# The root of every norm as one power on GpSimd, in a hybrid decoder layer

## The chip, the core and the metric

The kernel runs on one core of a Trainium2 chip. A core has five engines with their own instruction queues: TensorE (PE in the profile; its weight loads are PEld), VectorE (DVE), ScalarE (ACT), GpSimd (POOL) and SyncE (SP), which here issues the DMAs. Each queue is worked off in order, and queues wait for each other through semaphores. The metric is the device time of one execution in microseconds (us); lower is better.

## The reference

One decoder layer on x of 1024 tokens by 1024 channels: a gated feed-forward half step, a mixer of two head groups (a gated short convolution and a diagonal state space model), a second feed-forward half step, and a final norm. What matters here is that every part starts with a root mean square norm over the channels of a token:

```python
def rms_norm(x, gain):
    xf = x.astype(jnp.float32)
    y = xf * lax.rsqrt(jnp.mean(xf * xf, axis=-1, keepdims=True) + EPS)
    return (y * gain.astype(jnp.float32)).astype(x.dtype)

x = x + 0.5 * g1 * swiglu(modulate(rms_norm(x, ffn1_norm), sh1, sc1), ...)
h = modulate(rms_norm(x, mix_norm), sh2, sc2)          # -> conv branch, ssm branch
y_mix = concatenate([rms_norm(y_conv, out_norm_conv), rms_norm(y_ssm, out_norm_ssm)])
x = x + g2 * (y_mix @ w_out)
x = x + 0.5 * g3 * swiglu(modulate(rms_norm(x, ffn2_norm), sh3, sc3), ...)
return rms_norm(x, final_norm)
```

So there are six norms: before the first feed-forward, before the mixer, one for each head group's output, before the second feed-forward, and at the end. Each needs one value per token, 1/sqrt(mean + 1e-6).

## The kernel before

Channels lie on the 128 partitions and tokens along the free axis, in two halves of 512 tokens. Every matrix product is done with both operands split into a high and a low part (three matmuls per product, `mm3`), so TensorE has some 7500 matmuls of 128x128 by 512. Weights come by DMA into `raw`, ScalarE casts the high part `w`, VectorE subtracts to get the low part; GpSimd adds and subtracts weight blocks (`sums`, `raw`) for the blocks that are multiplied with seven products instead of eight.

A norm goes through five steps, each on another engine. ScalarE squares the channel tiles, GpSimd and VectorE add the squares (tiles named `..q`); TensorE multiplies the sum with a column of ones, which leaves the sum of squares of 512 tokens as 128 partitions by 4 columns in `st`; `roots` turns `st` into the inverse root `y` (128x4); `wide` copies each column of `y` 128 times into `rb` (128x512); `spread` multiplies `rb` with the identity on TensorE, so that `bc` holds the root of each token on all partitions; then VectorE multiplies the channel tiles with `bc`. `Sumsq.rstd` puts `stats` (the sums, `roots` and `wide`) a few ticks behind its cause, and `spread` another 7 or 11 ticks behind that; one tick is one `mm3`. These are the due times by which the author places the steps between the matmuls.

`roots` on VectorE before the change: one instruction makes v = st/width + eps (`..nv`). Then eight small ones on 128x4: a first guess from the bits of v as an integer (`ni`), and two polynomial steps (`na`, `ny`), the last of which leaves y larger by 1/0.375; the factor 0.375 is applied in `wide`.

There are 13 calls. Two are in the prologue (`root_of(0)` and `root_of(1)`, names `p0..` and `p1..`), where the tokens lie on the partitions and the result `py` is used by ScalarE and GpSimd themselves to scale the token rows `xb`, before TensorE transposes them (`pt`); there a ninth small instruction multiplies by 0.375. Then one for each half: `n2a`, `n2b` (mixer norm), `nAa`, `nAb` (convolution output), `nBa`, `nBb` (state space output), `n3a`, `n3b` (second feed-forward). The final norm has three: `n_0_0` for the first half, and `n_1_0` and `n_1_256` for two quarters of the second (the profile cuts the numbers and shows them as `n_0..` and `n_256..`).

The order on each engine is that of the source in the prologue (`InOrder.strict`); behind it a scheduler orders the instructions of each engine by their dependences and its own estimate of durations. A long side job shares the engines with the matmuls: 56 products of a weight tile `wm` with the condition vector (`mod_tile`, one VectorE instruction of 128x1024 and one accumulator read), each of which frees one of two buffers and so lets SyncE issue the next `wm` load.

Of the kernel before, what the change touches and what calls it, by code (L numbers as in the profile page):

```python
# [13 lines left out]
F32 = mybir.dt.float32  # L14
F32R = mybir.dt.float32r
I32 = mybir.dt.int32
AF = mybir.ActivationFunctionType
ALU = mybir.AluOpType
# [3 lines left out]
P = 128  # L22
D = 1024
# [29 lines left out]
RC2 = float(np.float32(np.round((TWO_PI - RC1) * 2.0**20) / 2.0**20))  # L53
RC3 = float(np.float32(TWO_PI - RC1 - RC2))
ROUND = 12582912.0
ROOT_BITS, ROOT_A, ROOT_B = 1595932665.0, 0.703952253, 2.38924456
EXP_C = [1.9875691500e-4, 1.3981999507e-3, 8.3334519073e-3, 4.1665795894e-2, 1.6666665459e-1, 5.0000001201e-1]


# [176 lines left out]
def hymba_layer(ctx: ExitStack, tc, x_d, xt_d, wm1_d, wmod_d, gu1_d, gs1_d, ds1_d, wl1_d, win_d, wout_d, glu_d, gu2_d, gs2_d, wd2_d, ds2_d, wl2_d, cols_d, cond_d, lam_d, bc_d, out_d):  # L236
    nc = tc.nc
    V, A, T, SP = (InOrder(tc, e) for e in (nc.vector, nc.scalar, nc.tensor, nc.sync))

    def pool(name, bufs=1, **kw):  # L240
        return ctx.enter_context(tc.tile_pool(name=name, bufs=bufs, **kw))
# [3 lines left out]
    const = pool("const", side="right")  # L245
# [26 lines left out]
    def t2k(name):  # L272
        return tmp.tile([P, HALF], F32, tag="t", name=name)
# [3 lines left out]
    make_identity(nc, ident[:])  # L277
    one = const.tile([P, 1], F32, name="one")
    V.memset(one[:], 1.0)
    mods = const.tile([P, 3, KT], F32, name="mods")  # L280
    scl = const.tile([P, 3, KT], F32, name="scl")
    gate = const.tile([P, 3, KT], F32, name="gate")
# [73 lines left out]
    class Sumsq:  # L356
# [28 lines left out]
        def rstd(self, width, use, wait=4, wait2=7):  # L385
            q = self.n // P

            def stats():
                st = sm([P, 4], self.name + "st")
                self.sums(st)  # L390
                y = roots(st, q, width, self.name)
                rb = wide(y, self.name)
                clock.after(wait2, lambda: use(spread(rb, self.name)))

            clock.after(wait, stats)

    def roots(st, q, width, nm):

        v, y, a = (const.tile([P, 8], F32, tag=f"n{i}", name=f"{nm}n{i}", bufs=1)[:, :q] for i in "vya")
        yi = const.tile([P, 8], I32, tag="ni", name=nm + "ni", bufs=1)[:, :q]  # L400
        V.tensor_scalar(out=v, in0=st[:, :q], scalar1=1.0 / width, scalar2=EPS, op0=ALU.mult, op1=ALU.add)
        V.tensor_scalar(out=yi, in0=v.bitcast(I32), scalar1=-0.5, scalar2=ROOT_BITS, op0=ALU.mult, op1=ALU.add)
        src = yi.bitcast(F32)
        V.scalar_tensor_tensor(out=a, in0=src, scalar=-ROOT_A, in1=src, op0=ALU.mult, op1=ALU.mult)
        V.tensor_tensor(out=a, in0=a, in1=v, op=ALU.mult)
        V.scalar_tensor_tensor(out=y, in0=a, scalar=ROOT_A * ROOT_B, in1=src, op0=ALU.add, op1=ALU.mult)
        V.tensor_tensor(out=a, in0=y, in1=y, op=ALU.mult)
        V.tensor_tensor(out=a, in0=a, in1=v, op=ALU.mult)
        V.scalar_tensor_tensor(out=a, in0=a, scalar=-10.0 / 3.0, in1=a, op0=ALU.add, op1=ALU.mult)
        V.scalar_tensor_tensor(out=y, in0=a, scalar=5.0, in1=y, op0=ALU.add, op1=ALU.mult)  # L410
        return y

    widened = []
# [1 line left out]
    def wide(y, nm):  # L415

        q = y.shape[1]
        rb = t2k(nm + "rb")[:, : q * P].rearrange("p (a b) -> p a b", a=q)
        r = V.tensor_scalar(out=rb, in0=y.unsqueeze(2).to_broadcast([P, q, P]), scalar1=0.375, scalar2=None, op0=ALU.mult)
        widened.append(r)  # L420
        return rb

# [399 lines left out]
    st = t2k("st")  # L822
# [48 lines left out]
    root = [None, None]  # L871

    def root_of(h):
        y = roots(st[:, 4 * h : 4 * h + 4], 4, D, f"p{h}")
        root[h] = t2k(f"py{h}")[:, :4]
        V.tensor_scalar(out=root[h], in0=y, scalar1=0.375, scalar2=None, op0=ALU.mult)

    def scaled(h, lo, hi, engine=A):

# [68 lines left out]
    mod_load()  # L948
    kept_busy(4, ident[:], xb[0][:, :HALF])
    root_of(0)  # L950
    scaled(0, 0, 2)
    mods_of(0)
# [13 lines left out]
    squares(7, V)  # L966
    scaled(0, 2, 8)
    root_of(1)
    scaled(1, 0, 2)
    scaled(1, 2, 4, nc.gpsimd)  # L970
# [928 lines left out]
```

## Time and profile before

| | before |
|---|---|
| time, three runs | 1700.83, 1701.79, 1703.76 us (median 1701.79) |
| profiled execution | span 1704.7 us; the page gives no other time for it |
| TensorE busy, weight loads | 98%, 80% of the span |
| VectorE, ScalarE, GpSimd busy | 74%, 37%, 22% |
| DMA | 281 MB, mean 165 GB/s |
| TensorE clock granted | 0.9 or more of full speed in each of 40 slices |

All times of the trace below are inside the 1704.7 us span, which is 2.9 us above the median of the runs. Rows of a timeline give the start, the duration, the engine, the line, the operation, the tile written and the tiles read, shapes and a count; the bracket gives the idle time of that engine just before, and what ended it. Nearly all operations have the line of one helper (L112), so tiles tell them apart.

### The profile page before, as it was taken

How to read it: one execution, taken by the hardware profiler on the slowest of the kernel's cores; microseconds unless marked ns; L12 is line 12 of the kernel's file. 1: busy time of each engine (PE TensorE's matmuls, PEld its weight loads, DVE VectorE, ACT ScalarE, POOL GpSimd, SP SyncE). 2: the span in 40 equal slices, each digit the busy share in tenths (PEclk: the TensorE clock that was granted, in tenths of full speed). 3: DMA queues.
4: the chain of work that ended last, by engine and by line, in shares of the span. 5: the costliest groups of instructions: out<-in, count | busy, mean ns of one | idle time of the engine just before them, and what ended most of it. 6: DMA issues, size and time to landing. Idle time of an engine off the chain costs nothing.

```text
span 1704.7 us, 20844 instructions
## 1 busy us (share of the span) xinstructions
PE 1666.8 (98%) x7545; PEld 1369.9 (80%) x7545; DVE 1255.5 (74%) x1957; ACT 630.1 (37%) x1064; POOL 382.0 (22%) x297
## 2 busy tenths in 40 slices
PE   8999999999999999999999999999999999999997
PEld 5888877788878888788777878888888888888886
DVE  7897899998589978735555857957767667576655
ACT  6525323333354332331113415434344434322233
POOL 1012222242222412100000021122333223333212
PEclk9999999999999999999999999999999999999999
DMA  8544454544665448244654232324443343759212
GB/s 350 187 148 137 172 189 155 183 149 139 213 216 170 151 152 291 70 111 149 191 151 134 70 129 112 112 74 182 188 174 148 148 173 148 269 228 381 110 50 99
DMA packets 101625, 281.48 MB, mean 165 GB/s; under 512 B 19345, under 2 KB 34961, under 8 KB 90386
## 3 DMA queue, kind: packets, MB, share of 16 engines
q1 hardware_dynamic: 101522, 280.15, 46.6%
q8 instruction: 59, 0.97, 0.2%
q14 instruction: 44, 0.36, 0.1%
HBM read 195.69 MB, written 76.02 MB: 159 GB/s over the span
## 4 chain that ended last, share of the span: by engine, by line
PE 70%; DVE 8%; DMA 5%; issue 1%; ACT 0%; SPq 0%; POOL 0%; DVEq 0%; ACTq 0%; POOLq 0%
PE wo L112 4%; PE fald L112 3%; PE fb10d L112 2%; PE u L112 2%; PE fbd_1B L112 2%; PE fbd_0B L112 2%; DMA swz<-si 2%; DVE w L112 2%; PE fad_1B L112 2%; PE b L112 2%; PE fad_0B L112 1%; PE c L112 1%; PE fb0u L112 1%; PE fad_1C L112 1%; PE fbd_1C L112 1%; PE fbd_0C L112 1%
## 5 line engine op out<-in xcount | busy, mean ns | idle before, releaser
L112 ACT CAST w<-raw 128x512 fp32r<-128x512 f32 (+1 forms) x374 | 240.9, 677 | 497.7 <-issue 72.7
L112 DVE TENSOR_TENSOR w<-raw,w 128x512 fp32r<-128x512 f32 (+1 forms) x374 | 311.2, 851 | 101.2 <-ACT w L112 100.6
L177 POOL TENSOR_TENSOR raw<-sums,raw 128x512 f32<-128x512 f32 x54 | 81.6, 1511 | 420.9 <-DVE w L112 419.9
L168 POOL TENSOR_TENSOR sums<-raw 128x512 f32<-128x512 f32 x54 | 76.4, 1415 | 308.1 <-DMA raw<-in_ds 129.1
L179 POOL TENSOR_TENSOR raw<-raw 128x512 f32<-128x512 f32 x54 | 82.3, 1526 | 86.6 <-DVE w L112 86.0
L112 DVE CUSTOM_DVE_ANT_0 wm<-wm,cact 128x1024 f32<-128x1024 f32 x56 | 77.7, 1407 | 15.1 <-DMA wm<-in_wmod 15.0
L169 POOL TENSOR_TENSOR raw<-raw 128x512 f32<-128x512 f32 x54 | 85.2, 1577 | 4.2
L370 POOL TENSOR_TENSOR n3aq<-n3aq,n3aq 128x512 f32<-128x512 f32 x5 | 7.5, 1499 | 277.4 <-ACT n3aq L112 277.2
L112 DVE TENSOR_TENSOR w<-sums,w 128x512 fp32r<-128x512 f32 x54 | 54.9, 1029 | 3.4 <-ACT w L112 2.8
L112 PE MATMUL p<-h,w 128*128 128x512 f32 x192 | 49.4, 407 | 2.0 <-ACT h L112 1.5
L112 PE MATMUL wo<-oa,w 128*128 128x512 f32 x192 | 45.5, 391 | 2.1 <-ACT w L112 1.3
L112 PE MATMUL c<-h,w 128*128 128x512 f32 x192 | 47.1, 397 | 0.0
L112 PE MATMUL v<-h,w 128*128 128x512 f32 x192 | 46.9, 395 | 0.0
L112 PE MATMUL b<-h,w 128*128 128x512 f32 x192 | 45.6, 393 | 0.0
L112 PE MATMUL wo<-ob,w 128*128 128x512 f32 x192 | 45.2, 391 | 0.0
L112 PE MATMUL u<-h,w 128*128 128x512 f32 x192 | 44.8, 392 | 0.2 <-DVE h L112 0.2
L112 PEld LDWEIGHTS wo<-oa,w 128*128 128x128 f32 x192 | 35.8, 188 | 10.2 <-ACT w L112 1.7
L112 PEld LDWEIGHTS p<-h,w 128*128 128x128 f32 x192 | 35.7, 192 | 10.1 <-ACT h L112 2.0
L112 ACT CAST w<-sums 128x512 fp32r<-128x512 f32 x54 | 32.7, 619 | 28.8 <-PE fa10gE L112 2.5
L112 PEld LDWEIGHTS u<-h,w 128*128 128x128 f32 x192 | 35.7, 188 | 8.3 <-DVE h L112 0.6
L112 PEld LDWEIGHTS wo<-ob,w 128*128 128x128 f32 x192 | 35.8, 188 | 7.4
L112 PEld LDWEIGHTS c<-h,w 128*128 128x128 f32 x192 | 35.8, 190 | 7.2
(1579 smaller groups left out, 4039.8 us busy)
## 6 DMA issues: line engine op xcount, KB each, us to landing
raw<-in_gs SPq DMA_DIRECT2D x38, 1024.0 KB, 5.0
wm<-in_wmod SPq DMA_DIRECT2D x56, 512.0 KB, 5.2
raw<-in_ds SPq DMA_DIRECT2D x16, 1024.0 KB, 6.6
mw<-in_wm SPq DMA_DIRECT2D x8, 1024.0 KB, 8.4
raw<-in_win SPq DMA_DIRECT2D x8, 1024.0 KB, 5.5
raw<-in_gu SPq DMA_DIRECT2D x6, 1024.0 KB, 4.9
raw<-in_wl SPq DMA_DIRECT2D x5, 1024.0 KB, 6.7
xb<-in_xt SPq DMA_DIRECT2D x8, 512.0 KB, 6.4
```

The source lines that it names most:

```text
L112: r = getattr(self.engine, name)(*args, **kw)
L168: self.G.tensor_tensor(out=f, in0=r[2], in1=r[1], op=ALU.subtract)
L169: self.G.tensor_tensor(out=r[1], in0=r[1], in1=r[0], op=ALU.subtract)
L177: self.G.tensor_tensor(out=r, in0=s["t3"], in1=r, op=ALU.add)
L179: self.G.tensor_tensor(out=r, in0=self.chunk(j, 3), in1=r, op=ALU.subtract)
L370: nc.gpsimd.tensor_tensor(out=a, in0=a, in1=sq[:, :n], op=ALU.add)
```

## The change

Of `roots` only the first instruction (v) stays on VectorE. The eight others are replaced by one GpSimd instruction that raises v to the power of a constant tile `power` (128x4, filled with -0.5 once at the start). The factor in `wide` becomes 1.0, with the instruction kept, and in the prologue the power writes `py` itself, so the ninth instruction goes too. Over the 13 calls 106 VectorE instructions leave, 13 GpSimd instructions and one fill come.

```diff
+    power = const.tile([P, 4], F32, name="power")
+    nc.gpsimd.memset(power[:], -0.5)
...
-    def roots(st, q, width, nm):
+    def roots(st, q, width, nm, y=None):
...
         V.tensor_scalar(out=v, in0=st[:, :q], scalar1=1.0 / width, scalar2=EPS, op0=ALU.mult, op1=ALU.add)
-        V.tensor_scalar(out=yi, in0=v.bitcast(I32), scalar1=-0.5, scalar2=ROOT_BITS, op0=ALU.mult, op1=ALU.add)
-        src = yi.bitcast(F32)
-        V.scalar_tensor_tensor(out=a, in0=src, scalar=-ROOT_A, in1=src, op0=ALU.mult, op1=ALU.mult)
-        V.tensor_tensor(out=a, in0=a, in1=v, op=ALU.mult)
-        V.scalar_tensor_tensor(out=y, in0=a, scalar=ROOT_A * ROOT_B, in1=src, op0=ALU.add, op1=ALU.mult)
-        V.tensor_tensor(out=a, in0=y, in1=y, op=ALU.mult)
-        V.tensor_tensor(out=a, in0=a, in1=v, op=ALU.mult)
-        V.scalar_tensor_tensor(out=a, in0=a, scalar=-10.0 / 3.0, in1=a, op0=ALU.add, op1=ALU.mult)
-        V.scalar_tensor_tensor(out=y, in0=a, scalar=5.0, in1=y, op0=ALU.add, op1=ALU.mult)
+        nc.gpsimd.tensor_tensor(out=y, in0=v, in1=power[:, :q], op=ALU.pow)
         return y
...
-        r = V.tensor_scalar(out=rb, in0=y.unsqueeze(2).to_broadcast([P, q, P]), scalar1=0.375, scalar2=None, op0=ALU.mult)
+        r = V.tensor_scalar(out=rb, in0=y.unsqueeze(2).to_broadcast([P, q, P]), scalar1=1.0, scalar2=None, op0=ALU.mult)
...
     def root_of(h):
-        y = roots(st[:, 4 * h : 4 * h + 4], 4, D, f"p{h}")
         root[h] = t2k(f"py{h}")[:, :4]
-        V.tensor_scalar(out=root[h], in0=y, scalar1=0.375, scalar2=None, op0=ALU.mult)
+        roots(st[:, 4 * h : 4 * h + 4], 4, D, f"p{h}", root[h])
```

The scheduler moves other instructions with it. At the mixer norm's second half, TensorE works on the projection `u` between the sums `n2bst` and the spread `n2bbc`. Before:

```order
L112 MATMUL n2bst<-one,n2bq_5670 128x1 x4
L112 MATMUL u_0_5992<-h_0_5897,w_5971 128x512 x3
L112 MATMUL u_0_5991<-h_0_5905,w_5947 128x512 x3
L112 MATMUL u_0_5992<-h_0_5905,w_5971 128x512 x3
L112 MATMUL u_0_5990<-h_0_5913,w_5888 128x512
L112 MATMUL n2bbc<-ident,n2brb 128x128 x4
```

And with the change:

```order
L111 MATMUL n2bst<-one,n2bq_5650 128x1 x4
L111 MATMUL u_0_5963<-h_0_5868,w_5942 128x512 x3
L111 MATMUL u_0_5962<-h_0_5876,w_5918 128x512 x3
L111 MATMUL n2bbc<-ident,n2brb 128x128 x4
L111 MATMUL u_0_5963<-h_0_5876,w_5942 128x512 x3
```

The spread now stands behind 6 matmuls of `u` instead of 10.

In the output projection (`wo`), VectorE's queue has the updates of x, the low parts of the weights `w`, and the side products `wm`. Before, from the last tile of the modulation vector `mods` on (ISA is the product):

```order
L112 ISA wm_3_1_7994,mods<-wm_3_1_7994,cact_7300 128x1024
L112 ISA mods 128x1
L112 TENSOR_TENSOR mods<-mods,cols 128x8
L112 SCALAR_TENSOR_TENSOR x_1_3918<-wo_1_7808,gate,x_1_3918 128x512
L112 SCALAR_TENSOR_TENSOR x_1_3918<-wo_1_7809,gate,x_1_3918 128x512
L112 TENSOR_TENSOR w_7967<-raw_7520,w_7967 128x1024
L112 TENSOR_TENSOR w_7970<-raw_7520,w_7970 128x1024
L112 ISA wm_0_0_8006,gate<-wm_0_0_8006,cact_7300 128x1024
```

And with the change:

```order
L111 TENSOR_TENSOR mods<-mods,cols 128x8
L111 ISA wm_0_0_7932,gate<-wm_0_0_7932,cact_7262 128x1024
L111 ISA gate 128x1
L111 SCALAR_TENSOR_TENSOR x_1_3898<-wo_1_7743,gate,x_1_3898 128x512
L111 SCALAR_TENSOR_TENSOR x_1_3898<-wo_1_7744,gate,x_1_3898 128x512
L111 TENSOR_TENSOR w_7893<-raw_7473,w_7893 128x1024
L111 TENSOR_TENSOR w_7896<-raw_7473,w_7896 128x1024
L111 ISA wm_0_1_7945,gate<-wm_0_1_7945,cact_7262 128x1024
```

The product of each `wm` tile stands earlier by one place among the x updates and weights, here and down to the last tile `wm_2_1` of this stretch.

At the end VectorE has the last x updates from `fb10d`, the multiplications with `bc`, and the small steps of `n_1_0` between them. Before:

```order
L112 TENSOR_TENSOR x_0_3917<-x_0_3917,n_0_0bc 128x1024
L112 SCALAR_TENSOR_TENSOR n_1_0ny<-n_1_0na,n_1_0ni 128x2
L112 SCALAR_TENSOR_TENSOR x_1_3921<-fb10d_1_256_13449,gate,x_1_3921 128x256
L112 TENSOR_TENSOR n_1_0na<-n_1_0ny 128x2
L112 TENSOR_TENSOR n_1_0na<-n_1_0na,n_1_0nv 128x2
L112 SCALAR_TENSOR_TENSOR n_1_0na<-n_1_0na 128x2
L112 SCALAR_TENSOR_TENSOR n_1_0ny<-n_1_0na,n_1_0ny 128x2
L112 TENSOR_SCALAR n_1_0rb<-n_1_0ny 128x256
L112 TENSOR_TENSOR x_1_3918<-x_1_3918,n_1_0bc 128x2x256
L112 TENSOR_TENSOR x_1_3919<-x_1_3919,n_1_0bc 128x2x256
L112 TENSOR_SCALAR n_1_256nv<-n_1_256st 128x2
```

And with the change:

```order
L111 SCALAR_TENSOR_TENSOR x_1_3900<-fb10d_1_256_13288,gate,x_1_3900 128x256
L111 TENSOR_SCALAR n_1_0rb<-n_1_0ny 128x256
L111 TENSOR_TENSOR x_0_3896<-x_0_3896,n_0_0bc 128x1024
L111 SCALAR_TENSOR_TENSOR x_1_3901<-fb10d_1_256_13319,gate,x_1_3901 128x256
L111 TENSOR_TENSOR x_0_3897<-x_0_3897,n_0_0bc 128x1024
L111 SCALAR_TENSOR_TENSOR x_1_3901<-fb10d_1_256_13339,gate,x_1_3901 128x256
L111 TENSOR_TENSOR x_1_3898<-x_1_3898,n_1_0bc 128x2x256
L111 TENSOR_SCALAR n_1_256nv<-n_1_256st 128x2
L111 TENSOR_TENSOR x_1_3899<-x_1_3899,n_1_0bc 128x2x256
L111 TENSOR_SCALAR n_1_256rb<-n_1_256ny 128x256
```

`n_1_0rb` now stands ahead of the last two x updates, and the last root's first step `n_1_256nv` stands behind one multiplication with `n_1_0bc` instead of two.

More of the change, by code (lines that the diff above doesn't have):

```diff
@@ L55 @@
 ROUND = 12582912.0
-ROOT_BITS, ROOT_A, ROOT_B = 1595932665.0, 0.703952253, 2.38924456
 EXP_C = [1.9875691500e-4, 1.3981999507e-3, 8.3334519073e-3, 4.1665795894e-2, 1.6666665459e-1, 5.0000001201e-1]
@@ L395, in rstd @@
             clock.after(wait, stats)
-    def roots(st, q, width, nm):
-        v, y, a = (const.tile([P, 8], F32, tag=f"n{i}", name=f"{nm}n{i}", bufs=1)[:, :q] for i in "vya")
-        yi = const.tile([P, 8], I32, tag="ni", name=nm + "ni", bufs=1)[:, :q]
+    def roots(st, q, width, nm, y=None):
+        v = const.tile([P, 8], F32, tag="nv", name=nm + "nv", bufs=1)[:, :q]
+        if y is None:
+            y = const.tile([P, 8], F32, tag="ny", name=nm + "ny", bufs=1)[:, :q]
         V.tensor_scalar(out=v, in0=st[:, :q], scalar1=1.0 / width, scalar2=EPS, op0=ALU.mult, op1=ALU.add)
-        V.tensor_scalar(out=yi, in0=v.bitcast(I32), scalar1=-0.5, scalar2=ROOT_BITS, op0=ALU.mult, op1=ALU.add)
-        src = yi.bitcast(F32)
-        V.scalar_tensor_tensor(out=a, in0=src, scalar=-ROOT_A, in1=src, op0=ALU.mult, op1=ALU.mult)
-        V.tensor_tensor(out=a, in0=a, in1=v, op=ALU.mult)
-        V.scalar_tensor_tensor(out=y, in0=a, scalar=ROOT_A * ROOT_B, in1=src, op0=ALU.add, op1=ALU.mult)
-        V.tensor_tensor(out=a, in0=y, in1=y, op=ALU.mult)
-        V.tensor_tensor(out=a, in0=a, in1=v, op=ALU.mult)
-        V.scalar_tensor_tensor(out=a, in0=a, scalar=-10.0 / 3.0, in1=a, op0=ALU.add, op1=ALU.mult)
-        V.scalar_tensor_tensor(out=y, in0=a, scalar=5.0, in1=y, op0=ALU.add, op1=ALU.mult)
+        nc.gpsimd.tensor_tensor(out=y, in0=v, in1=power[:, :q], op=ALU.pow)
         return y
```

## The prediction

> **What bounds the kernel now.** I read the page first, then the chain of waits, then the timeline round each of the 13 roots.
>
> ```profile
> span 1704.7 us, 20844 instructions
> PE 1666.8 (98%) x7545; PEld 1369.9 (80%) x7545; DVE 1255.5 (74%) x1957; ACT 630.1 (37%) x1064; POOL 382.0 (22%) x297
> PE 70%; DVE 8%; DMA 5%; issue 1%; ACT 0%; SPq 0%; POOL 0%; DVEq 0%; ACTq 0%; POOLq 0%
> ```
>
> TensorE sets the time: 70% of the span on the chain, VectorE 8%. So taking 106 small VectorE instructions out (about 0.2 us apart each) saves nothing in general. A root counts only where TensorE stands still for it, or where its path to the first or last result is bare. For most roots it doesn't stand still, because the spread is placed 7 ticks behind the sums. The tightest I find of these is nAa (timeline, and the view of its tile):
>
> ```profile
> 901.64 0.16 DVE L112 TENSOR_SCALAR nAanv<-nAast 128x4 f32<-128x4 f32 x1
> 904.45 0.43 DVE L112 TENSOR_SCALAR nAarb<-nAany 128x512 f32<-128x512 f32 x1
> L112 PEld LDWEIGHTS nAabc<-ident,nAarb x8: 187/192/192, 906.1 to 907.0; 128*128 128x128 f32 x8
> ```
>
> rb ends at 904.88 and TensorE reads it at 906.1: the root is hidden with 1.2 us to spare. n2a, nBa, nBb, n3a and n3b read the same way. Five places are left: p0, p1, n2b, nAb and the three roots of the end.
>
> **The price of the power.** No row of the trace has a power on GpSimd. Call its time X, start to end. Its neighbours are the adds that run while VectorE is quiet (groups kept apart by shape):
>
> ```profile
> L370 POOL TENSOR_TENSOR n_0q<-n_0q,n_0q 128x512 f32<-128x512 f32 x6 | 7.7, 1290 | 48.5 <-ACT n_0q L112 48.5
> L370 POOL TENSOR_TENSOR n_256q<-n_256q,n_256q 128x256 f32<-128x256 f32 x6 | 4.4, 737 | 4.8 <-ACT n_256q L112 4.8
> ```
>
> 1290 - 737 = 553 ns for 256 elements is 2.16 ns an element, and 737 - 553 = 184 ns is the fixed part. A 128x4 add would take 0.19 us; that is the low end, since a power can't be less work than an add. The high end I take from the longest of these rows, 1.29 us, with nothing that strictly forbids more. I take X = 0.75, the middle: the shape is next to the low end, the arithmetic isn't. The handover is 0.18 us from VectorE to GpSimd (py ends at 23.51, GpSimd starts at 23.69, below), and 0.04 from an engine to the next as from py to ScalarE (23.55). So the new root takes 0.17 + 0.18 + X + 0.04 = 0.39 + X from the start of v to its reader, and the old one some 2 us.
>
> **The prologue, p0.**
>
> ```profile
> 4.10 0.65 SPq L112 DMA_DIRECT2D raw<-in_gu  x1
> raw<-in_gu SPq DMA_DIRECT2D x1, 1024.0 KB, 10.2
> 10.82 0.17 DVE L112 TENSOR_SCALAR p0nv<-st 128x4 f32<-128x4 f32 x1
> 12.86 1.71 ACT L112 ACTIVATE xb<-xb,py 128x256 f32<-128x256 f32 x4 [3.56 <-issue]
> 14.48 1.04 ACT L112 CAST w<-raw 128x1024 fp32r<-128x1024 f32 x1
> ```
>
> ScalarE would start xb at 10.82 + 0.39 + X = 11.21 + X instead of 12.86, 0.9 us earlier at X = 0.75. But the next thing in its queue, the cast of the first weight, needs raw, which lands at 4.10 + 10.2 = 14.3. So ScalarE gains 0.15 us at most; it loses when 12.83 + X passes 14.48, at X = 1.65.
>
> **The prologue, p1.**
>
> ```profile
> 8.15 0.33 SPq L112 DMA_DIRECT2D mw<-in_wm  x1
> mw<-in_wm SPq DMA_DIRECT2D x1, 1024.0 KB, 13.6
> 21.56 0.17 DVE L112 TENSOR_SCALAR p1nv<-st 128x4 f32<-128x4 f32 x1
> 23.34 0.17 DVE L112 TENSOR_SCALAR py<-p1ny 128x4 f32<-128x4 f32 x1
> 23.55 1.71 ACT L112 ACTIVATE xb<-xb,py 128x256 f32<-128x256 f32 x4 [0.22 <-DVE py L112]
> 23.69 1.86 POOL L885 TENSOR_SCALAR xb<-xb,py 128x256 f32<-128x256 f32 x1 [22.41 <-DVE py L112]
> 24.69 1.49 DVE L112 CUSTOM_DVE_ANT_0 mw<-mw,cact,cols 128x1024 f32<-128x1024 f32 x1
> L112 DVE CUSTOM_DVE_ANT_0 mw<-mw,cact,cols x8: 1273/1280/1490, 14.0 to 52.8; 128x1024 f32<-128x1024 f32 x8
> ```
>
> ScalarE was idle only 0.22 us here, so 0.22 is all p1 can give; it loses when X passes 23.33 - 21.95 = 1.38. Both gains reach TensorE's start, from which it runs without a break: 0.37 us in all at X = 0.75.
>
> One thing speaks against it. Behind v the queue now has the product of mw, with two inputs in SBUF, and mw lands at 8.15 + 13.6 = 21.75, when the power comes at 21.91 (0.15 earlier with p0's gain): a toss-up which is first. The rows show what meeting costs: xb on GpSimd took 1.86 us where a two-input add of that size takes 0.74, and the product that began meanwhile took 1.49 against a median of 1.28. [...]
>
> **n2b.**
>
> ```profile
> 720.42 2.58 PE L112 MATMUL u<-h,w 128*128 128x512 f32 x10
> 720.60 0.16 DVE L112 TENSOR_SCALAR n2bnv<-n2bst 128x4 f32<-128x4 f32 x1 [1.14 <-PE n2bst L112]
> 722.86 0.97 PEld L112 LDWEIGHTS n2bbc<-ident,n2brb 128*128 128x128 f32 x8 [0.30 <-DVE n2brb L112]
> ```
>
> The 10 matmuls left 0.30 us of waiting. The order moves the spread up to behind 6; four at 2.58 - 0.30 over 10, 0.23 us each, are 0.91 us, so TensorE is at the spread at 722.86 - 0.30 - 0.91 = 721.65. rb takes 0.43 and 0.04 to be seen: it is there at 720.60 + 0.39 + X + 0.47 = 721.46 + X, which is 722.21. Wait 0.56 instead of 0.30: a loss of 0.25 us (0.5 - X as a gain). The scheduler has placed this spread for a cheap power.
>
> **nAb.** In the chain of waits VectorE goes from the root straight to yg, for which TensorE stands still (the last row is TensorE's timeline):
>
> ```profile
> 923.09 0.17 DVE nAbnv L112
> ...
> 924.68 0.07 DVE nAbny L112
> ...
> 925.08 0.70 DVE yg L112
> ...
> 925.83 9.55 PE L112 MATMUL gl<-yg,w 128*128 128x512 f32 x29 [1.73 <-DVE yg L112]
> ```
>
> The root isn't needed for yg; it only stood before it in the queue. Without eight instructions yg starts 924.84 - 923.25 = 1.59 us earlier, less than the 1.73 that TensorE idles. The power reads SBUF just then, at 923.43, and may keep yg out for X: the gain is between 1.59 - 0.75 = 0.84 and 1.59. I take the middle, 1.2.
>
> **The output projection.** VectorE waits for wm tiles here with the x updates and weights behind them, and TensorE pays:
>
> ```profile
> 988.78 1.23 DVE L112 CUSTOM_DVE_ANT_0 wm<-wm,cact 128x1024 f32<-128x1024 f32 x1 [3.50 <-DMA wm<-in_wmod]
> 993.96 2.09 DVE L112 CUSTOM_DVE_ANT_0 wm<-wm,cact 128x1024 f32<-128x1024 f32 x1 [1.49 <-DMA wm<-in_wmod]
> 998.44 1.63 PE L112 MATMUL wo<-oa,w 128*128 128x512 f32 x6 [1.32 <-ACT w L112]
> 1000.80 7.80 PE L112 MATMUL wo<-oa,w 128*128 128x512 f32 x33 [0.74 <-DVE w L112]
> ```
>
> Each product frees the buffer for the next load, so products one place earlier start their loads earlier, and less stands behind a late one. Up to 1.32 + 0.74 = 2.06 us can come back; none of it, if a load stays late. I take half, 1.0.
>
> **The end.**
>
> ```profile
> 1690.19 0.88 PE L112 MATMUL fb10d<-fb_1a,w 128*128 128x256 f32 x6
> 1691.85 0.47 DVE L112 SCALAR_TENSOR_TENSOR x<-fb10d,gate,x 128x256 f32<-128x256 f32 x1
> 1693.42 0.71 PE L112 MATMUL n_0bc<-ident,n_0rb 128*128 128x128 f32 x4 [2.35 <-DVE n_0rb L112]
> 1693.97 0.95 PE L112 MATMUL n_256st<-one,n_256q 128*128 128x1 f32 x8
> 1694.17 1.28 DVE L112 TENSOR_TENSOR x<-x,n_0bc 128x512 f32<-128x512 f32 x2 [0.80 <-PE n_0bc L112]
> 1695.38 0.15 DVE L112 TENSOR_SCALAR n_256nv<-n_256st 128x2 f32<-128x2 f32 x1
> 1697.21 0.29 DVE L112 TENSOR_SCALAR n_256rb<-n_256ny 128x256 f32<-128x256 f32 x1
> 1697.55 1.22 PE L112 MATMUL n_256bc<-ident,n_256rb 128*128 128x128 f32 x4 [2.63 <-DVE n_256rb L112]
> ```
>
> TensorE is through at 1691.07 and then idles 2.35 and 2.63 us for two roots. With the change n_1_0's rb is done before the last x updates, so its spread no longer holds up the sums n_256st behind it; the last x update comes 0.2 us earlier, the sums at about 1692.7 instead of 1693.97 and done at 1693.65; v of the last root stands behind one multiplication (half of 1.28) instead of two and starts at 1693.67. Then 0.34 to the power, X, 0.04: rb at 1694.05 + X = 1694.8 against 1697.21, a gain of 2.4 us. Since each of the three powers delays the next, I estimate that the gain falls by 2 us for each us of X: 3.9 - 2X.
>
> **The sum.** 0.37 - 0.25 + 1.2 + 1.0 + 2.4 = 4.7 us off the profiled span, 1704.7 to 1700.0; off the median of the runs, 1701.8 to **1697.1 us**. The copies in `wide` keep their cost; the fill of `power` is off the path by 9 us.
>
> **Rivals.**
> A, slower: the power is long. From X = 1.65 on the prologue gives 3.25 - 2X (each of p0 and p1 past its margin), so the sum is 3.25 - 2X + 0.5 - X + 1.2 + 1.0 + 3.9 - 2X = 9.85 - 5X, which turns at X = 2.0: five bare powers in line. At X = 3 it is -5.2, **1707.0**. For it: nothing in the trace bounds the arithmetic of a power. Against: 16 times the fixed part.
> [...]
> C, hidden anyway: the wm loads stay late (-1.0), yg is kept out (-0.36) and the loads hold the prologue (-0.37): 3.0 left, **1698.8**, no change that can be told.
> D, the power is as cheap as an add (X = 0.19): 0.37 + 0.3 + 1.5 + 1.0 + 2.7 = 5.9, **1695.9**. The end is then bound by VectorE's multiplications.
>
> **The numbers.** 0.2%, 3.4 us, is about what a measurement of this kernel can tell from no change. Chances: the forecast 0.40 (0.33 faster, 0.07 same, since X up to 1.3 belongs to it), A 0.22 (0.19 slower, 0.03 same), D 0.13 (faster), B 0.10 (half each), C 0.15 (0.03 faster, 0.12 same). Faster 0.54, same 0.27, slower 0.19. The forecast's own range is 1695.5 to 1699. The whole range goes from 1694.5 (D with all of the 2.06) to 1706.0 (A up to X = 2.8).
>
> **What would show it.** The power's rows give X at once. p0: ScalarE's cast of w at 14.3 with an idle time in front. p1: xb 0.3 to 0.4 earlier, or behind a product. n2b: TensorE's wait before the spread, 0.56. nAb: the wait for yg below 0.9. Output projection: the 1.32 and 0.74 smaller. End: from the last fb10d matmul to the end of the span 2.4 us shorter. I'm wrong if X is past 2, or if TensorE waits for a spread that was hidden (nAa, n2a and the others give way at X of some 3.6).

## The result: 1.8% slower, and the loss is in TensorE's matmuls

| | before | with the change |
|---|---|---|
| median of the runs | 1702.78 us | 1732.72 us |
| ratio, 95% interval | | 1.0177 (1.0161 to 1.0193) |
| profiled span | 1704.7 us | 1731.8 us |
| TensorE busy | 1666.8 us | 1705.0 us |

The forecast was 1697.1 us, within 1694.5 to 1706. The kernel lost 30 us instead of winning 5, and none of the rivals comes near. One of the twelve runs of e7 below had a granted clock of 0.75 and took 2085 us; medians and ratios leave it out. The head of the page of the changed kernel:

```profile
span 1731.8 us, 20768 instructions
PE 1705.0 (98%) x7545; PEld 1368.6 (79%) x7545; DVE 1236.5 (71%) x1851; ACT 632.4 (37%) x1064; POOL 394.5 (23%) x311
PE 73%; DVE 6%; DMA 4%; issue 1%; ACT 0%; POOL 0%; SPq 0%; DVEq 0%; POOLq 0%; ACTq 0%
```

TensorE has the same 7545 matmuls and is busy 38 us longer. VectorE's share of the chain fell from 8% to 6%, as the change meant it to. So where is the time? I set the first weight load of the same tiles beside each other in both traces (the times between are worked out from the trace; all in us):

| stretch, from tile to tile | before | change | difference |
|---|---|---|---|
| start to `n2ast` (prologue, first feed-forward) | 693.8 | 704.8 | +11.0 |
| `n2ast` to `nAbst` | 228.2 | 229.3 | +1.1 |
| `nAbst` to `nBast` | 22.7 | 18.9 | -3.8 |
| `nBast` to `n3bst` | 103.4 | 106.5 | +3.1 |
| `n3bst` to `n_0st` (second feed-forward) | 629.7 | 648.0 | +18.3 |
| `n_0st` to the end | 26.8 | 24.3 | -2.5 |

The loss lies in the two feed-forward stretches, and the second has only the root of `n3b` at its start, for which TensorE doesn't stand still. The view of windows of that stretch, before and with the change (columns: window; busy time and count of TensorE, its weight loads, VectorE, ScalarE, GpSimd; granted clock; DMA):

```profile
core 0: us, PE busy (x) PEld busy (x) DVE busy (x) ACT busy (x) POOL busy (x), PEclk, DMA share, GB/s
1049.00:1676.00 627.00, 627.00 (x2773) 519.29 (x2774) 430.48 (x612) 236.19 (x413) 177.47 (x124) 1.00 0.44 166
```

```profile
1064.00:1704.00 640.00, 640.00 (x2749) 515.42 (x2748) 425.64 (x602) 236.49 (x411) 174.99 (x123) 1.00 0.42 161
```

TensorE is busy without a gap in both, at full clock in both. But 627 us hold 2773 matmuls (226.1 ns each), and 640 us only 2749 (232.8). Nothing waits; each matmul takes 6.7 ns more. The groups show it too, for one of the plainest, before and after (their 389 and 395 ns go from start to end of one matmul; neighbours overlap, so that a new one starts every 226 or 233 ns):

```profile
L112 PE MATMUL fb0g<-h,w 128*128 128x512 f32 x96 | 23.2, 389 | 0.0
```

```profile
L111 PE MATMUL fb0g<-h,w 128*128 128x512 f32 x96 | 23.9, 395 | 0.0
```

Nearly all operations of VectorE, ScalarE and GpSimd have kept their durations to 10 ns (the same join of both traces), and what differs adds up to some 1 us on each engine, so it's TensorE alone.

**What else the change moved.** The diff takes two tiles out of the pool `const` (`na` and `ni`, 128x8, 32 bytes per partition each) and puts one in (`power`, 16 bytes, which takes 32). `const` is the first of the pools that are laid from the top of the memory downwards (`side="right"`), so each pool below it moves up by 32 bytes. The built programs' allocations, in bytes within a partition:

```
pool                          before                   change
ringp (3 weight tiles)        202752, 210944, 219136   202784, 210976, 219168
rawp, tmp, xp, ring1b         right-hand side          each + 32
movA (moving operands h ...)  1536, 5632, ...          the same
ring1 (a 4th weight tile)     87552                    the same
```

The weights of nearly all matmuls now lie 32 bytes further, and what they are multiplied with doesn't. `ring1` is the exception, and it makes a test inside the changed kernel's own trace: for 48 matmuls in a row, from 65.83 us on, the weights come from `ring1`. Windows of the time just before, of the first eight of them and of the other 40:

```profile
62.08:65.81 3.73, 3.73 (x17) 3.01 (x16) 3.73 (x8) 1.55 (x3) 0.00 (x0) 1.00 0.91 328
65.81:67.66 1.85, 1.85 (x9) 1.50 (x8) 1.85 (x4) 1.85 (x4) 0.00 (x0) 1.00 0.19 78
67.66:76.73 9.07, 9.07 (x41) 7.51 (x40) 5.95 (x9) 1.62 (x2) 1.61 (x2) 1.00 0.61 220
```

By the weight loads: 16 in 3.73 us are 233 ns each, 8 in 1.85 us are 231, and 40 in 9.07 us are 227 each. Same kernel, same line, same moving operands; only the weights' address differs. Why the first eight don't have the full gain yet is open.

### The profile page after: what moved, and what is told of

It reads as the page before. It is cut to its first block, busy times and chain, and to the rows that moved or that the text cites. A ratio compares the mean times of both kernels' runs of the same rounds, so it can differ in the third digit from the quotient of the medians.

```text
span 1731.8 us, 20768 instructions
## 1 busy us (share of the span) xinstructions
PE 1705.0 (98%) x7545; PEld 1368.6 (79%) x7545; DVE 1236.5 (71%) x1851; ACT 632.4 (37%) x1064; POOL 394.5 (23%) x311
## 4 chain that ended last, share of the span: by engine, by line
PE 73%; DVE 6%; DMA 4%; issue 1%; ACT 0%; POOL 0%; SPq 0%; DVEq 0%; POOLq 0%; ACTq 0%
PE fald L111 4%; PE wo L111 3%; PE fb10d L111 2%; PE fbd_1B L111 2%; PE fbd_0B L111 2%; PE u L111 2%; PE fad_1B L111 2%; PE fad_0B L111 2%; PE b L111 2%; DMA swz<-si 1%; PE fb0u L111 1%; PE fbd_1C L111 1%; PE fbd_1A L111 1%; PE fbd_0A L111 1%; PE fb0d L111 1%; PE fad_1C L111 1%
## 5 line engine op out<-in xcount | busy, mean ns | idle before, releaser
L111 PEld LDWEIGHTS b<-h,w 128*128 128x128 f32 x192 | 35.6, 188 | 8.1
```

What stands on the lines that cost most here:

```text
L111: r = getattr(self.engine, name)(*args, **kw)
```

## The experiments

T1 is the theory that addresses cost the 30 us. R1 (the power itself, or its meeting with others) and R2 (the scheduler's new order) are its rivals. Start-to-start times are means over the 128x512 matmuls that follow each other without a wait, worked out from the trace. Ratios are to the kernel before in the same set of runs, with a 95% interval.

**e1: the change at the old addresses.**

```diff
-PAD = 96, 100
+PAD = 96, 108
```

`PAD` holds the sizes of two filler tiles, one at each end of the memory. Eight more elements give `const` its 32 bytes back.

> The changed kernel with the right-hand filler tile 32 bytes longer (PAD 96, 108), so that every right-hand pool, the ring of weight tiles among them, lies at the addresses it had before; the instructions and their order are those of the change. Theory T1 (the loss is the address: removing two small tiles and adding one moved the weight tiles by 32 bytes, and a matmul whose weights lie there takes 6.5 ns more): the 128x512 matmuls go back to 389 ns, and the kernel is faster than before by what the prediction's terms give at the measured power of 1.02 us, 3.8 us: about 1698.5 us, 1696 to 1701. Rival R1 (the power on GpSimd, or its meeting with other readers, slows the stretches): 1732, matmuls at 396 ns. Rival R2 (the scheduler's new order costs it): 1732 too, with the matmuls at 396 ns or with waits of TensorE.

Measured: 1697.53 us against 1701.33, ratio 0.9979 (0.9967 to 0.9991); matmuls 227 ns from start to start, `fb0g` back at 389. The whole loss is gone and the gain is there. Since the instructions and their order are the change's, R1 and R2 fall.

**e2: the kernel before at the new addresses.**

```diff
-PAD = 96, 100
+PAD = 96, 92
```

> The kernel before, eight small operations on VectorE and all, with the right-hand filler 32 bytes shorter (PAD 96, 92), so that the right-hand pools lie where the change has put them. T1: 128x512 matmuls at 396 ns instead of 389, and the whole loss without any power: 1702.8 + some 31 us (the 30 us lost and the few that the root gives back), 1729 to 1738 us. R1 and R2: no change from before, 1701 to 1705 us, 389 ns.

Measured: 1736.16 us, ratio 1.0199 (1.0178 to 1.0220), 233 ns. Its group:

```profile
L112 PE MATMUL fb0g<-h,w 128*128 128x512 f32 x96 | 23.9, 396 | 0.0
```

34.8 us lost with no power anywhere; with the 3.8 that e1 wins, 31.0, and the change lost 30. T1 stands.

**e3 and e4: which address?** e3 is the change with `PAD = 96, 92` (the right-hand side 64 bytes above the old place), e4 the change with `PAD = 104, 108` (the right-hand side at the old place, the left-hand one, with the moving operands, 32 bytes up).

> The changed kernel with the filler 32 bytes shorter (PAD 96, 92): the right-hand pools lie 64 bytes above their addresses before, the ring at 64 past a multiple of 1024. T1 as a matter of 64-byte pieces: the same as with the old addresses, about 1698.5 us, 389 ns. T1 as a matter of exact multiples of 1024 (or of these addresses alone): slow, about 1732 us, 396 ns. R1, R2: 1732 us.

> The changed kernel with the right-hand pools at their old addresses and the left-hand filler 32 bytes longer (PAD 104, 108): now the moving operands (the split activations h, and the kept ones) lie 32 bytes past a multiple of 64, the ring's three right-hand weight tiles don't. T1w (only the weights' address counts): 389 ns and 1698 to 1700 us, a little over the aligned one for the one weight slot that lies on the left for a time. T1b (any operand that TensorE reads): 396 ns or more, about 1732 us. R1, R2: 1732 us.

Measured: e3 1734.20 us (1.0187, 1.0165 to 1.0209), e4 1732.60 us (1.0177, 1.0157 to 1.0198). In each expectation the case named first was fast, and both are slow. So it isn't that weights must begin at a multiple of 64 bytes: in e3 they do, and in e4 they haven't moved at all. In e4 the one weight tile on the left, `ring1`, has moved together with its moving operands, and its matmuls keep 227 ns but for the first, where the others take 233. That suggests the difference of the two addresses.

**e5: both sides moved by 32 bytes.**

```diff
-PAD = 96, 100
+PAD = 104, 100
```

> The changed kernel with the right-hand pools where the change put them (PAD right 100, weights 32 bytes past a multiple of 64) and the left-hand pools 32 bytes further too (PAD left 104, moving operands 32 past as well). In the runs so far the one weight tile that lies on the side of the moving operands (ring1) kept 227 ns a matmul in every kernel, and the others took 233 whenever one side alone was moved, by 32 or by 64 bytes. T1d (only the difference between the weights' and the moving operand's address counts, which is a multiple of 512 again here): 227 ns from start to start, about 1697.5 us. T1a (each must lie at a good address of its own): 233 ns or more, 1732 us or above.

Measured: 1701.10 us, ratio 0.9990 (0.9978 to 1.0002), 227 ns. Here each operand lies where it was slow in another kernel, and together they are fast:

```profile
L111 PE MATMUL fb0g<-h,w 128*128 128x512 f32 x96 | 23.2, 389 | 0.0
```

Only the difference counts. That e5 wins a little less than e1 I can't explain; the intervals overlap.

**e6: the matmuls alone.** Nothing of the layer is computed; one weight tile, one moving tile, no other engine at work.

```diff
+SETS = (
+    [(0, w) for w in (0, 32, 64, 96, 128, 160, 192, 224, 256, 320, 384, 448, 480, 512)]
+    + [(32, 0), (32, 32), (64, 0), (64, 64), (128, 0), (128, 128), (256, 0), (256, 256), (0, 0)]
+)
...
+        hi, lo = (wt[:, q + w // 4 + k * P : q + w // 4 + (k + 1) * P] for q in (0, 2048))
+        ah, al = (mv[:, q + m // 4 : q + m // 4 + HALF] for q in (0, 1024))
+        T.matmul(out, lhsT=hi, rhs=ah, start=True, stop=False)
+        T.matmul(out, lhsT=hi, rhs=al, start=False, stop=False)
+        T.matmul(out, lhsT=lo, rhs=ah, start=False, stop=True)
```

> Only matmuls, nothing of the layer (the output isn't computed): after 300 to warm up, 23 groups of 96 of the kernel's form (high and low parts in turn, 128x512), in the name of each the bytes by which the moving operand (m) and the weights (w) are moved from a common base that is a multiple of 128. Nothing else runs beside them. T1d: 227 ns from start to start (a group in 21.8 us) in m0w0, m0w512, m32w32, m64w64, m128w128, m256w256, and 233 (22.4 us) or more in m0w32, m0w64, m32w0, m64w0; between 64 and 512 it shows the period. If the slower ones need traffic of other engines, all groups are alike. If the absolute address counts, m32w32 and m64w64 are slow too.

The groups (one of the three lines of each; the name has the bytes by which the moving operand, m, and the weights, w, are shifted):

```profile
L84 PE MATMUL m0w0x<-mv,wt 128*128 128x512 f32 x32 | 12.4, 389 | 0.0
L84 PE MATMUL m0w32x<-mv,wt 128*128 128x512 f32 x32 | 12.7, 395 | 0.0
L84 PE MATMUL m0w64x<-mv,wt 128*128 128x512 f32 x32 | 12.7, 396 | 0.0
L84 PE MATMUL m0w128x<-mv,wt 128*128 128x512 f32 x32 | 12.6, 394 | 0.0
L84 PE MATMUL m0w256x<-mv,wt 128*128 128x512 f32 x32 | 12.4, 389 | 0.0
L84 PE MATMUL m32w0x<-mv,wt 128*128 128x512 f32 x32 | 12.6, 395 | 0.0
L84 PE MATMUL m32w32x<-mv,wt 128*128 128x512 f32 x32 | 12.4, 389 | 0.0
L84 PE MATMUL m64w64x<-mv,wt 128*128 128x512 f32 x32 | 12.4, 389 | 0.0
```

The mean from start to start within a group, by the difference w - m modulo 256 bytes:

| w - m, bytes | 0 | 32 | 64 | 96 | 128 | 160 | 192 | 224 |
|---|---|---|---|---|---|---|---|---|
| ns | 226.7 to 227.0 | 233.3 | 233.4 | 234.2 | 232.3 to 232.5 | 233.4 | 228.9 to 229.0 | 233.3 to 233.4 |

Groups with the same remainder agree within 0.4 ns, whichever operand was moved and however far (m0w64 and m0w320 both have 233.4, m0w192, m0w448 and m64w0 229.0, 228.9 and 228.9). So, at the offsets tried and for matmuls of this form: with nothing else running, a stream of them costs 2.5 to 3.3% more (1% at 192) unless the weights' address and the moving operand's differ by a multiple of 256 bytes. Why, the traces don't tell. They show that weights are loaded while TensorE is busy (519.29 of the 627 us and 515.42 of the 640 us in the two windows of the result), and not what the one does to the other.

**e7 and e10: the power twice.**

```diff
         nc.gpsimd.tensor_tensor(out=y, in0=v, in1=power[:, :q], op=ALU.pow)
+        nc.gpsimd.tensor_tensor(out=y, in0=v, in1=power[:, :q], op=ALU.pow)
```

at the old addresses. This asks whether the prediction's terms have the right slope.

> The changed kernel at the old addresses (PAD 96, 108) with each power done twice in a row, the same result written again: the time of a root goes from X = 1.02 us to some 2.04; TensorE's order is the same, VectorE's but for one place. The prediction's terms: at X = 1.02 a gain of 3.9 us, at 2.04 a loss of 0.35, so 4.3 us slower than with one power, about 1701.8 us against 1697.5; the end alone 2 us longer, TensorE's wait before n2bbc 1.0 us longer. Rival (the roots are covered, the gain comes from VectorE's queue alone): within 1 us of 1697.5.

Measured: ratio 1.0021 (1.0007 to 1.0034), about 1706.3 us, 7 us slower than with one power instead of 4.3. Where these went is read from e10, the same kernel run once more for a profile.

> The kernel with each power done twice, at the old addresses, for its profile: it was some 7 us slower than with one power where the prediction's terms gave 4.3. By the terms TensorE's wait before n2bbc is 1.0 us longer, the end 2 us, nAb and the prologue 1.3. Rival: a place that the prediction took for hidden (nAa, n2a, nB, n3, up to a root of 3.6 us) has begun to hold TensorE.

Its span is 1705.4 us, 7.5 over e9 below. Stretch by stretch against e9: start to the last matmul of `p` +3.2, from there to `n2ast` +1.3, TensorE's wait before `n2bbc` 1.83 instead of 0.75, from `n2bbc` to `nAast` -1.0, `nAbst` to `nBast` the same, output projection +1.2, end +1.7. No term had the +1.3, the -1.0 and the +1.2, and I can't explain them. The prologue is the surprise that I can. GpSimd's timeline in e10 and then ScalarE's:

```profile
11.16 1.02 POOL L404 TENSOR_TENSOR py<-p0nv,power 128x4 f32<-128x4 f32 x1 [9.87 <-DVE p0nv L111]
12.25 1.90 POOL L405 TENSOR_TENSOR py<-p0nv,power 128x4 f32<-128x4 f32 x1
23.16 2.04 POOL L404 TENSOR_TENSOR py<-p1nv,power 128x4 f32<-128x4 f32 x1 [9.00 <-DVE p1nv L111]
25.27 1.13 POOL L405 TENSOR_TENSOR py<-p1nv,power 128x4 f32<-128x4 f32 x1
```

```profile
15.80 1.03 ACT L111 CAST w<-raw 128x1024 fp32r<-128x1024 f32 x1
26.44 1.71 ACT L111 ACTIVATE xb<-xb,py 128x256 f32<-128x256 f32 x4 [1.80 <-POOL py L405]
```

And VectorE's in the same kernel:

```profile
11.94 1.35 DVE L111 CUSTOM_DVE_ANT_0 mw<-mw,cact,pre 128x1024 f32<-128x1024 f32 x1 [0.94 <-DMA mw<-in_wm]
22.98 1.34 DVE L111 CUSTOM_DVE_ANT_0 mw<-mw,cact,pre 128x1024 f32<-128x1024 f32 x1
```

The two powers that began while VectorE's product was under way (from 11.94 to 13.29, from 22.98 to 24.32) ended 0.86 and 0.88 us after the product did (12.25 + 1.90 = 14.15, 23.16 + 2.04 = 25.20). So the two roots of the prologue are 3.0 and 3.24 us long, not 2.04. With these, the prediction's own margins give 12.83 + 3.0 - 14.48 = 1.35 and 3.24 - 1.38 = 1.86, 3.2 together. Against e9 the cast of `w` starts 1.34 us later (15.80 instead of 14.46), and the last matmul of `p` 3.2 us later. So the power was held there by a product; with one power this has no occasion in the prologue: in e9 the product of p1 starts 0.11 us after the power (21.95 and 21.84), and both take their usual time (1.35 and 1.01 us). There is one occasion elsewhere, in the changed kernel's own trace:

```profile
954.29 0.68 DVE L111 TENSOR_TENSOR oa<-oat,oa 128x512 fp32r<-128x512 f32 x1
954.51 1.32 POOL L404 TENSOR_TENSOR nBany<-nBanv,power 128x4 f32<-128x4 f32 x1 [17.99 <-DVE nBanv L111]
```

This power began 0.22 us into a two-input operation of VectorE and ended 0.86 us behind it (955.83 and 954.97), as the two above do; TensorE doesn't wait for that root.

**e8 and e9: only the roots that pay.** e8 leaves n2a, n2b, nBa and nBb on VectorE, at the old addresses (`PAD = 96, 92`, since `na` and `ni` come back); e9 is e1 once more beside it.

```diff
+ON_VECTOR = ("n2a", "n2b", "nBa", "nBb")
...
+        if nm in ON_VECTOR:
...
+            return y
         nc.gpsimd.tensor_tensor(out=y, in0=v, in1=power[:, :q], op=ALU.pow)
```

> The changed kernel at the old addresses, with the roots of n2a, n2b, nBa and nBb left on VectorE as before (eight small operations, factor 0.375 in the widening) and the power for the nine others. TensorE's order is then that of the kernel before, and VectorE's in the output projection too. In the profiles so far the power costs 0.4 us at n2b (TensorE waits longer for the spread) and 1.8 us in the output projection (61.6 us from nBbst to n3ast become 63.4: a product of wm stands one place earlier, waits for its load and keeps ob from TensorE). Theory (each root is worth what its own stage shows): those 2.2 us come back, nAb (4.3) and the end (2.5 to 3) stay: 2 us below the changed kernel at the old addresses in the same set, 6 to 7 us below before, ratio 0.996. Rival (the stages pass their gains and losses on to each other, so only the sum of all roots counts): no better than the changed kernel at the old addresses.

> The changed kernel at the old addresses once more, for comparison in the same set: ratio 0.998 as before (0.9967 to 0.9991), 61.6 + 1.8 us from nBbst to n3ast, 18.5 us from nAbst to nBast against 22.7 before.

Measured: e8 1696.48 us, ratio 0.9958 (0.9944 to 0.9971); e9 1699.10 us, 0.9973 (0.9964 to 0.9982). 2.6 us between them where 2 were expected. The output projection (`nBbst` to `n3ast`) takes 61.65 us in e8, 63.3 in e9, 61.6 before; `nAbst` to `nBast` is 18.5 in both. So in the output projection the roots of that stage cost what it shows. e8 has the lowest median of its set; e11, the same instructions, has a ratio of 0.9971, so over a whole run e8's lead on e9 is less sure than the 1.7 us of that stage.

**e11: e8 with the right-hand side moved by 256 bytes.**

```diff
-PAD = 96, 92
+PAD = 96, 28
```

> The kernel with the roots of n2a, n2b, nBa and nBb on VectorE and the power for the rest, once more, with the right-hand filler 256 bytes shorter (PAD 96, 28 for 96, 92): the weights lie 256 bytes past a multiple of 1024, the moving operands 512 past. If the period is 256 bytes, as the groups of matmuls alone have it (226.7 ns at a difference of 0, 256 and 512 bytes), nothing changes: matmuls of 389 ns, ratio to before 0.996. If the kernel's matmuls need a multiple of 512, as the runs of whole kernels left open: 396 ns, 1727 us or so.

Measured: 1697.81 us, ratio 0.9971 (0.9957 to 0.9984), `fb0g` at 389 ns. A difference of 256 bytes is as good as none in the whole kernel too.

## Why the prediction was wrong, step by step

**The step that failed** is in the first part and isn't even written as a number: that TensorE sets the time and that the change reaches it only through waits. From there "it runs without a break" to the sum, every term is a wait of TensorE; the 7500 matmuls themselves were taken as fixed. "The fill of `power` is off the path by 9 us" is true of its time and forgets its place in memory. The cause is in the lines that allocate (`power` comes, `na` and `ni` go; the diff printed above shows only the first). A term for it would have been matmuls times ns: 6.7 ns over the 6863 matmuls of 128x512 whose weights moved are 46 us, of which TensorE's waits took up about 10 (its idle time, span less busy, is 37.9 us before and 28.2 in e2; 34.8 us of loss were measured in e2).

"From which it runs without a break" doesn't hold either. Between 137 and 580 us the kernel before has nine waits of TensorE of 0.46 to 1.62 us, 8.8 us in all, and the changed kernel has six there, 3.5 us in all. The longest before:

```profile
215.34 1.84 PE L112 MATMUL fa4gC<-h1S,w 128*128 128x512 f32 x7 [1.62 <-DVE fa4gt L112]
```

So a gain or a loss of TensorE in front of them need not reach the end as it is. And the margin of p1, 1.38 us, is where its gain begins to shrink; by the same rows it turns into a loss at 1.60, as the formula of rival A has it.

**The rest of the sum** can be checked at the old addresses (e1, e9), against the profile of before; gains in us:

| term | predicted | by its formula at X = 1.02 | measured |
|---|---|---|---|
| prologue | 0.37 | 0.37 | 0.4 to 0.6 |
| n2b | -0.25 | -0.52 | -0.45 |
| nAb | 1.2 | 0.57 to 1.59 | 4.3 |
| output projection | 1.0 | 1.0 | -1.7 to -1.9 |
| end | 2.4 | 1.9 | 2.9 |
| sum | 4.7 | 3.8 | 5.4 |

The whole difference of medians is 3.8 (e1) and 4.3 us (e9); two stretches without a term make the rest uncertain: from `n2bbc` to `nAast`, between 176 and 179 us in these three profiles, and from the last matmul of `p` to `n2ast`, 1.0 and 1.8 us shorter than before in e1 and e9. The forecast of 4.7 would have stood at the old addresses, but by luck: two of its terms were wrong by 3 us each, one way and the other.

*The price.* The view of the power's line in the changed kernel (duration min/median/max, first and last start):

```profile
L404 POOL TENSOR_TENSOR py<-p0nv,power x1: 1019/1019/1019, 11.8 to 11.8; 128x4 f32<-128x4 f32 x1
L404 POOL TENSOR_TENSOR nBany<-nBanv,power x1: 1319/1319/1319, 954.5 to 954.5; 128x4 f32<-128x4 f32 x1
L404 POOL TENSOR_TENSOR n_256ny<-n_256nv,power x1: 707/707/707, 1723.1 to 1723.1; 128x2 f32<-128x2 f32 x1
```

1.02 us for 128x4 and 0.71 for 128x2: 0.155 us an element and 0.40 fixed, worked out from these two. The 1.32 of nBa is the one beside `oa`. I took 0.75, within the 0.19 to 1.29 that I kept open. Rival A (X past 2) and D (0.19) are out.

*n2b.* The wait before the spread, by the weight loads, was 0.30 and is, in the changed kernel:

```profile
733.44 0.97 PEld L111 LDWEIGHTS n2bbc<-ident,n2brb 128*128 128x128 f32 x8 [0.75 <-DVE n2brb L111]
```

Right in sign and, at the measured X, in size (0.83 by the formula).

*nAb.* yg starts 1.6 us earlier, the top of what I gave. The lower value, 0.84, has the power keep yg out, which no run shows: in e9 the power runs from 922.06 to 923.07, yg begins at 922.15, and its seven operations take 4.31 us, with 4.30 before. TensorE's wait is nearly gone (e1):

```profile
920.51 6.87 PE L111 MATMUL gl<-yg,w 128*128 128x512 f32 x29 [0.15 <-DVE yg L111]
```

But the 29 matmuls behind the wait take 6.87 us instead of 9.55. Windows of the kernel before from the wait on, and then of e9 at the same place:

```profile
924.00:926.00 2.00, 0.27 (x2) 0.18 (x2) 1.62 (x7) 0.25 (x1) 0.00 (x0) 0.69 0.93 379
926.00:928.00 2.00, 2.00 (x5) 1.61 (x6) 2.00 (x4) 0.00 (x0) 0.00 (x0) 0.50 0.93 297
928.00:930.00 2.00, 2.00 (x6) 1.52 (x6) 1.72 (x4) 0.00 (x0) 0.00 (x0) 0.50 0.41 168
930.00:932.00 2.00, 2.00 (x7) 1.56 (x6) 0.00 (x0) 0.00 (x0) 0.00 (x0) 0.60 0.00 0
```

```profile
922.00:924.00 2.00, 1.85 (x9) 1.20 (x8) 1.84 (x4) 0.91 (x2) 1.01 (x1) 1.00 0.97 410
924.00:926.00 2.00, 2.00 (x11) 1.62 (x10) 2.00 (x5) 0.00 (x0) 0.00 (x0) 1.00 0.93 279
```

The column behind GpSimd's count is the granted clock. After the wait TensorE ran at half speed for some 7 us; in e9, without the wait, it doesn't. So 2.7 of the 4.3 us are clock and 1.6 are wait. e2, with the same order as before, has the same wait (1.72 us), a shorter fall, and 8.58 us for the 29 matmuls. But the wait alone doesn't bring the fall. Here is a longer one of e1, as TensorE's row and as windows:

```profile
137.67 2.55 PE L111 MATMUL fa2gC<-h1S,w 128*128 128x512 f32 x10 [1.89 <-DVE fa2gt L111]
136.00:138.00 2.00, 0.33 (x2) 0.32 (x3) 2.00 (x5) 1.98 (x4) 1.92 (x2) 1.00 0.15 32
138.00:140.00 2.00, 2.00 (x10) 1.65 (x9) 2.00 (x5) 1.99 (x4) 0.77 (x2) 1.00 0.17 35
```

The clock stays at 1.00. What decides is open, so how much of the 2.7 us every execution loses is open too. The term was right in mechanism and took only the wait.

*Output projection.* I had taken the products' move by one place as a gain, since their loads start earlier. e9's VectorE and weight loads show the other side:

```profile
965.61 1.48 DVE L111 CUSTOM_DVE_ANT_0 wm<-wm,cact 128x1024 f32<-128x1024 f32 x1 [1.69 <-DMA wm<-in_wmod]
967.02 2.05 DVE L111 SCALAR_TENSOR_TENSOR obt<-yb,cols,nBbbc 128x512 f32<-128x512 f32 x3
```

```profile
968.46 0.30 PEld L111 LDWEIGHTS wo<-ob,w 128*128 128x128 f32 x2 [0.97 <-ACT ob L111]
969.73 2.36 PEld L111 LDWEIGHTS wo<-ob,w 128*128 128x128 f32 x11 [0.97 <-DVE ob L111]
```

A product that stands one place earlier waits 1.69 us for its load with `obt` behind it in VectorE's queue, and TensorE waits twice 0.97 us for `ob`: 1.9 us, with no such wait before. The two waits that I meant to save, 1.32 and 0.74, are still there in e1 (1.34 and 0.72): the loads stayed late, rival C's case. e8, which restores the order, takes these 1.7 us back.

*The end.* e9's TensorE:

```profile
1687.01 0.61 PE L111 MATMUL n_0bc<-ident,n_0rb 128*128 128x128 f32 x4
1687.98 0.38 PE L111 MATMUL n_256st<-one,n_256q 128*128 128x1 f32 x2 [0.35 <-POOL n_256q L371]
1690.76 1.22 PE L111 MATMUL n_256bc<-ident,n_256rb 128*128 128x128 f32 x4 [1.36 <-DVE n_256rb L111]
```

The 2.35 us of waiting for the first spread are gone, the 2.63 for the last are 1.36; from the start of the last fb10d weight load to the end it's 11.1 us instead of 14.0. Right in mechanism. The formula's 1.9 us at X = 1.02 are 1.0 too few. A doubled power cost 1.7 us here, not 2, which gives 0.3 of that; TensorE no longer waits for the first spread (no wait before the first row); the rest isn't resolved.

## What to carry to other kernels

Before costing a change by its instructions, compare the addresses of the tiles that it doesn't name: a tile more or less in the first pool of a side moves every pool behind it, and a matmul of 227 ns became one of 233 because weights and moving operand no longer differed by a multiple of 256 bytes. When a busy engine's group means shift by the same few ns everywhere, while no wait grows, ask for the layout first; undoing the layout alone (e1) and doing it alone (e2) settles it in two runs. A wait of TensorE can cost more than its length, where the clock falls behind it (1.6 and 2.7 us here), and a step moved earlier in a queue gains only if its data are there (1.69 us of waiting for a load in e9, and 1.9 of TensorE behind it).

## What was unexpected of the hardware

**Two operand addresses interact.** 226.7 to 227.0 ns at a difference of 0, 256 or 512 bytes, 228.9 to 234.2 at all others tried, at full clock and with no other engine at work (e6). That is 2.2 to 7.5 ns more for each matmul.

**Half the clock after 1.7 us of waiting, but not each time.** The kernel before fell to a granted clock of 0.50 behind a wait of 1.73 us, and again behind one of 2.41 (at 818.61), and e2 behind one of 1.72; the kernel before kept 1.00 behind 1.62 us (at 215.34) and e1 behind 1.89.

**A power and a two-input product on VectorE.** When the product began first, the power took 1.90 and 2.04 us instead of 1.02 (e10); when the power began 0.1 us first, neither was held (1.01 and 1.35 us, e9).
